# Linear attention beside weight products: a head's small TensorE work in seven groups instead of fifteen half steps

## The chip, the core and the metric

The kernel runs on one core of one Trainium2 chip. The metric is the device time of one execution in microseconds (us). Engines are named as in the profile: PE is TensorE's matmuls, PEld its weight loads, DVE VectorE, ACT ScalarE, POOL GpSimd, SP SyncE, whose queue issues most DMAs. A line such as L543 is line 543 of the kernel before; the change keeps the line numbers.

## The reference

One step of a hybrid decoder layer for 528 prompt tokens (512 and 16 learned meta tokens) and 32 sample tokens (8 sequences of 4), in float32, with a model width of 1024:

```
h = x + 0.5 * rms_norm(swiglu(rms_norm(x, ffn1_pre_g), ...), ffn1_post_g)
proj = rms_norm(h, mix_pre_g) @ w_in
q_a, k_a, v_a, gk_low, r_a, q_b, k_b, v_b, gate_a, gate_b = split(proj)
g = log_sigmoid(gk_low @ w_gk2 + b_gk) / 16
o_a, s_new = gla_branch(q_a, k_a, v_a, g, s0)       # linear attention, 4 heads
o_a = rms_norm(o_a, gla_norm_g) * silu(r_a)
o_b = sb_attend(q_b, keys, vals, sb_bias)           # stick-breaking attention, 16 heads
m = sigmoid(gate_a) * (o_a @ w_o_gla) + sigmoid(gate_b) * (o_b @ w_o_sb)
h = h + rms_norm(m @ w_out, mix_post_g)
y = h + 0.5 * rms_norm(swiglu(rms_norm(h, ffn2_pre_g), ...), ffn2_post_g)
```

The change touches only the linear attention (GLA). A head has 128 key and 256 value columns; tokens go in chunks of 64:

```
b = cumsum(g) in the chunk
q_in, k_in, k_end = q * exp(b), k * exp(-b), k * exp(b_last - b)
o = tril(q_in @ k_in.T) @ v + q_in @ S          # S: the state ahead of the chunk
S = exp(b_last) * S + k_end.T @ v
```

The 8 sample sequences do the same with their own states, which are inputs and outputs.

## The kernel before, in words

Activations lie turned (features on partitions, 560 token columns: 512 prompt, 32 sample, 16 meta). Every weight product is done as three matmuls: weights and activations are split in a high and a low part, and high x high, high x low and low x high are summed in PSUM (L728, L729, L731 in `tile_steps`). One **half step** is one of eight blocks of 128 input rows, over two halves of the tokens: six matmuls. After each half step `step()` runs what has come due in a list `todo`; `later(n, f)` puts `f` there for n half steps on. Everything small is put between the half steps in this way.

Over the four heads the kernel runs this loop: 16 half steps per head, eight for the head's queries and eight for its keys.

```
for hd, head in enumerate(HEADS):
    if hd:
        for n, f in HEADS[hd - 1].pieces():
            later(n + (hd == 1), f)
    ...
    if hd < 3:
        gla_gates(hd + 1, GATES, (0, 2, 3, 6))
    later(ROWS, head.rows)
    later(ROWS + 1, head.rows_out)
```

So in the loop of one head the **pieces** of the head ahead of it run, at the half steps of the table `OFF`. Head 0's pieces run one half step later than the table says. Head 3's pieces run in the first twenty half steps of the attention, whose Pair 0 makes its queries and keys there (eight half steps each).

The pieces that matter here, with the PE lines: scores of the prompt (L480, L483), `turned` (transposes of the keys, L437, L440), `sample_scores` (L511), `souts` (sample outputs from the old states, L531), `state0` to `state2` (L456, L459), `sums0` and `sums1` (L499, L502: a head's output), `sample_sum` (L560, L561), `sstate0` to `sstate3` (sample states, L543), and `turn0` to `turn2` (transposes of the normalised output, L592, L595). The names with `_out` read a product out of PSUM, on ACT (copies and scaled copies, L446, L465, L487, L513, L537, L601, L604) or DVE (the states, L175). `norm` squares and sums the outputs (ACT, L574, L577, L578), and `normed` scales them (ACT, L584).

Two more sets of small work stand in the loop. `head.rows` turns the head's values into rows (L377, L381, three PSUM tiles), and `rows_out` reads them out (ACT, L390, L393). `gla_gates` prepares the decay of the next head: `ranks` (two products, L312, read out on ACT, L313), `logs` (ACT, L317, L318), `sums` (DVE, a scan, L324), `exps` (ACT, L333 to L335). L706 and L1006 on ACT and the subtractions of `lo` on DVE split the coming weights. L2448 on ACT (`sums_hi`) casts sums of activations that are read back from DRAM.

**What sets the order.** PE, DVE, ACT and POOL run in the order in which the program's text emits instructions; SP's queue is ordered by a scheduler. PSUM has eight banks: four, by turns, for the weight products (`ps("acc")`), and a pool of **four buffers** for all small products (`ps()`). A new small tile takes the buffer of the fourth tile before it, and its first matmul waits until that has been read out. SBUF is one arena of 150 units; each `take` gets the next place from the byte table `PLACES`, so a changed order needs a new table.

Of the kernel before, what the change touches and what calls it, by code (L numbers as in the profile page):

```python
# [50 lines left out]


PLACES = bytes.fromhex("""
1e1218555a06420c505e52908e8070488a7a7e667668946a3264868c4c7c6038842a883462283c742672240a544e6e000292042c4a6c78823e2c
103c383a363047412d54565a0a5808443e424660067c8c0c34882c4c26247262842a742e1e0200146e824a786c123016921a36226a664890947a
32683c8e1e1880408a5a701003254e64277e86360e1a050428761b3e8a1f3a2318535c1c64360265700019260c0d4e1b017176283b5a64180038
3924231e0270190c1a36770d4e1876535b04013822715a5d641f1e0c1a707718100219384e712176645c1e0c5a702353100077183971763b6421
1e0c4e705323105a380c1a717776183a64651e23703818534e100e0c7684946c90788e6458468274167c7a4c500a88183c123008684a8c442c48
2e9270747a242a361e2c004c5a5d4823502e2036424b222a1e214b4d222a4c202d50511e4b5150224d1f201e212400301e50181c224b38373b36
393a19181b82667468603c5c14123e160690625a42501c442e4618887a84802d1b7e76947857153f6961673d928c0a72221e08200d4a13758317  # L60
49704c484b4d5d548e865c8a6e566a0e2d6c0c2c7c401910645570801a2a18847a54585c57562d888978795494725856768c0a2c187e9220221e
0428887824269046003234304e743a6862186053146612023b364a4c3f3e0848162c8209395c1e9238787e2a5a3626765618424c3c245d685428
4a60538c48666394881a14623f3e3a72501c22291e045d926078384a30342a2c7e58680a234e905c486654823a8c08282409636294885b551674
4604480032222047535a3e601e7802382e4a50665d429236194e3a5c764c9063088c82091c625e5672943c745b182e3846025406287e78926636
262458304c4a6888901676631214343a5b4e2b193802302a4e460a08573644555854423a3430061902265b2b425534522438503b262a060a5430
1b364e3a02192450570844425b2b19364e3402525618080a4630242e26292a2c4250380654025b1942242e34572938521a1c2c36024e30502a06
0a2d5b5d083418582c2a42245b072e38245256291c1806342a503a02542608240a4e3028504345341a3628065b2b4e420a303a0656072c2a3738
241c1934265402283a0845365c305e432e1a24454e37075b30585642062a2c1843191b4536383a5434025e5c1d4f565158282e0a0618424e5b08
0230024345560642262434580a36545c5e3a381c34360a1a58062e2c3a184f515e06323058011a54004a4c5c185e5a76622a28604a44423a3856
3e4e460234081c62560a60763663064a4c32625c525036185a5e320002463a441d08364a38421c4c345c0604621c080676604c56440a185c3a5a  # L70
1c0832065e424438585c08301a360a3a4c1c4656544b1a3208344a5d5c3022061e5848204a4442385c3a340b1a460a44080642304c1c32480a1e
203a54585632481a4a2c34634476602a246150280a26020462060801004460522200762e30634c1c02184e3e5a604246621a4a4c635e004d0405
18026260364b44764a4d395a18006e64108a1612687c787e6a740c7a408e8c88707284576726941e926d3406083266800a2c4a37829150140e4c
668648206c54828356242a28903a36573c8c60623e3d662d82804a37670822762c6e8e64661e339226670635949532080b8872706655847a0774
54610c0d41403f7e68426f0a778d658f46588a0706080b16124f747c3830548a104c3a780e423648866c267a142a9084822e5a1a24804a7e7288
683462662c2001187092527658604e5450563e466e0c7a5b8e1d65641a1e1c8c320822245a4243065f7a943d0402203c46181c26648f451e0008
225c1a03441f4006233c0a8f478e2028642400422202441c433c40235a03041a64245d0b5c0a461e5f42008f8e653e5a3d20040b64400226245c
4625416544428f3c0a8e40210222645c0425652400448f3c208e47400a0241465c5d5e24648e668874606c386834842e7e8a042c901800200e76
3c827c5430620a48725c0846108636784e5e06042818261e015c245a064600035c25282700245a05290403260424030025292826274206544e04
40033e241d28041a3c002c52137a8c18261c  # L80
""")


# [53 lines left out]
def hybrid_step(  # L137
# [15 lines left out]
    V, S, G, T = nc.vector, nc.scalar, nc.gpsimd, nc.tensor  # L153
# [20 lines left out]
    def stt(out, a, s, b, op0, op1):  # L174
        V.scalar_tensor_tensor(out=out, in0=a, scalar=s, in1=b, op0=op0, op1=op1)  # L175
# [125 lines left out]
    class Gates:  # L301


        def __init__(self, hd):
            self.hd = hd
# [39 lines left out]
    OFF = ((3, "scores spread"), (4, "scores_out turned"), (5, "turned_out souts sample_scores"), (6, "souts_out state0 skeys0"),  # L345
# [3 lines left out]

    class Head:  # L350


        def __init__(self, hd):
            self.hd, self.km, self.px = hd, {}, {}

        def load(self):

# [92 lines left out]
        def state(self, n):  # L450

            p = ps()
            if n == 0:
                self.owner = [take(512) for _ in range(3)]
                self.st = [self.owner[(j + 1) // 2][:, 256 * ((j + 1) % 2) : 256 * ((j + 1) % 2) + 256] for j in range(-1, 4)]
                T.matmul(p[:, :256], self.tl[NS:NTL, 256:384], self.tl[NS:NTL, :256], start=True, stop=True)  # L456
# [129 lines left out]

        def out_turned(self, e):

            p = self.po = ps()
            if e < 2:  # L590
                for j in range(4):
                    T.transpose(p[:, P * j : P * j + P], self.on[j // 2][:, 256 * (j % 2) + P * e : 256 * (j % 2) + P * e + P], ident)  # L592
            else:
                for e in range(2):
                    T.transpose(p[:, NS * e : NS * e + NS], self.on[2][:NS, P * e : P * e + P], ident[:NS, :NS])  # L595

        def out(self, e):
            hd, p = self.hd, self.po
            if e < 2:
                oa[hd, e] = take(NP + NS)  # L600
                S.activation(oa[hd, e][:, :NP], p, AF.Copy, scale=g_gla[:, e : e + 1])  # L601
            else:
                for e in range(2):
                    S.activation(oa[hd, e][:, NP:], p[:, NS * e : NS * e + NS], AF.Copy, scale=g_gla[:, e : e + 1])  # L604
                give(*self.on)
                for e in range(2):
                    later(1, lambda e=e: nc.sync.dma_start(oa_dram[2 * hd + e], oa[hd, e]))
                    later(6, lambda e=e: give(oa.pop((hd, e))))

        def pieces(self):  # L610
# [154 lines left out]
    def later(n, f):  # L765
        todo.append([n, f])
# [748 lines left out]
    with tc.manual_schedule(engines={E.PE, E.DVE, E.Activation, E.Pool}):  # L1515
# [277 lines left out]
        p = ps()  # L1793
        for j in range(5):
            n = P if j < 4 else NTL
# [702 lines left out]
    with tc.manual_schedule(engines={E.PE, E.DVE, E.Activation, E.Pool}):  # L2498
# [8 lines left out]
        starts, n = {}, -MIX0  # L2507
# [49 lines left out]
        for pr in range(8):  # L2557
            now, n, after = Pair(pr), BEGIN[pr + 1], BEGIN[pr + 2] if pr < 7 else BEGIN[8] + 18
# [25 lines left out]
        n, w0 = BEGIN[8], Weights(0)  # L2584
# [16 lines left out]
        n = 0  # L2601
# [29 lines left out]
        n = 8 * len(PAGES)  # L2631
# [43 lines left out]
        n = 0  # L2675
# [126 lines left out]
```

## Time and profile before

| | us |
|---|---|
| median of 3 runs | 1482.35 (1481.65 to 1482.51) |
| the profiled execution | 1483.2 |
| its span | 1481.5 |
| granted TensorE clock, mean | 0.999 |
| POOL busy in the span | 86.6 |
| mean DMA rate over the span | 127 GB/s |

The profile's page comes from one execution, 0.85 us above the median; its span is 1.7 us shorter than its time. The span is the frame of all instruction rows below, which give a start and a duration in us. PE's durations overlap, since matmuls are pipelined: the time from one start to the next is what a matmul takes. ACT and DVE instructions overlap by a little. The four heads' loops and the first half steps of the attention, which the change touches, lie from about 457 to 580 us.

### The profile page before, as it was taken

The numbers are of one execution on the slowest core, as the hardware profiler recorded it, in microseconds if no ns is written. First come the engines' busy times: TensorE is split into PE (matmuls) and PEld (weight loads), VectorE is DVE, ScalarE is ACT, GpSimd is POOL, SyncE is SP. The second block draws the span as 40 slices with busy tenths as digits, with TensorE's granted clock in tenths as the row PEclk, the third lists the DMA queues.
The fourth block names the chain that finished last, engine by engine and source line by source line (L and its number), as shares of the span: only waits on it lengthen the run. The fifth ranks groups of instructions, "written<-read, shape, count | busy, mean of one in ns | idle before, by whom it ended". The sixth has DMA issues, their size and how long they took to land.

```text
span 1481.5 us, 29805 instructions
## 1 busy us (share of the span) xinstructions
PE 1472.6 (99%) x11825; PEld 1426.8 (96%) x11825; DVE 1097.5 (74%) x1844; ACT 818.8 (55%) x1537; POOL 86.6 (6%) x175
## 2 busy tenths in 40 slices
PE   9999999999999999999999999999999999999998
PEld 8999999999999889999998999999999999999998
DVE  5888888855677866988887754776577888889544
ACT  7455545533565557777776544644564554545334
POOL 2000000000000111412211000000000000000000
PEclk9999999999999999999999999999999999999999
DMA  8133333324665787568687757335531333333243
GB/s 254 44 100 92 100 94 100 90 79 128 179 133 130 180 164 162 115 116 154 148 141 168 238 130 212 100 93 156 164 104 51 104 95 110 96 104 88 85 141 123
DMA packets 288541, 187.61 MB, mean 127 GB/s; under 512 B 10988, under 2 KB 266674, under 8 KB 288402
## 3 DMA queue, kind: packets, MB, share of 16 engines
q1 hardware_dynamic: 280706, 181.97, 46.5%
q0 software_dynamic: 7680, 3.74, 2.3%
q8 instruction: 93, 1.52, 0.4%
q14 instruction: 46, 0.38, 0.1%
q10 hardware_dynamic: 16, 0.00, 0.0%
HBM read 160.63 MB, written 25.03 MB: 125 GB/s over the span
## 4 chain that ended last, share of the span: by engine, by line
PE 95%; DVE 2%; ACT 1%; DMA 1%; issue 0%; DVEq 0%; SPq 0%; ACTq 0%
PE acc L1302 8%; PE acc L1301 8%; PE acc L1300 8%; PE acc L741 7%; PE acc L744 6%; PE acc L742 6%; PE acc L728 5%; PE acc L729 5%; PE acc L731 5%; PE acc L1079 4%; PE acc L1081 4%; PE acc L1080 4%; PE acc L1242 2%; PE acc L1239 2%; PE acc L1240 2%; PE ps L2105 1%
## 5 line engine op out<-in xcount | busy, mean ns | idle before, releaser
L172 DVE TENSOR_TENSOR room<-room,room 128x560 fp32r<-128x560 f32 (+14 forms) x464 | 300.9, 667 | 85.2 <-ACT room L1059 17.7
L172 DVE TENSOR_TENSOR lo<-raw,hi 128x1024 fp32r<-128x1024 f32 (+1 forms) x207 | 248.6, 1202 | 76.6 <-ACT hi L1006 39.3
L1302 PE MATMUL acc<-room,lo 128*128 128x280 f32 (+1 forms) x896 | 259.6, 290 | 0.0
L1300 PE MATMUL acc<-room,hi 128*128 128x280 f32 (+1 forms) x896 | 259.1, 289 | 0.0
L1301 PE MATMUL acc<-room,hi 128*128 128x280 f32 (+1 forms) x896 | 259.1, 289 | 0.0
L1006 ACT CAST hi<-raw 128x1024 fp32r<-128x1024 f32 x114 | 119.5, 1052 | 143.5 <-PE acc L1301 49.0
L728 PE MATMUL acc<-room,hi 128*128 128x280 f32 x608 | 173.1, 301 | 0.3 <-DVE room L175 0.3
L1300 PEld LDWEIGHTS acc<-room,hi 128*128 128x128 f32 x896 | 168.8, 188 | 0.0
L1302 PEld LDWEIGHTS acc<-room,lo 128*128 128x128 f32 x896 | 168.7, 188 | 0.0
L1301 PEld LDWEIGHTS acc<-room,hi 128*128 128x128 f32 x896 | 168.5, 188 | 0.0
L729 PE MATMUL acc<-room,hi 128*128 128x280 f32 x608 | 163.5, 288 | 0.0
L1079 PE MATMUL acc<-room,hi 128*128 128x280 f32 x476 | 141.7, 298 | 1.1 <-ACT acc L1069 1.0
L172 DVE TENSOR_TENSOR lo<-room,hi 128x1024 fp32r<-128x1024 f32 x106 | 101.2, 955 | 53.0 <-ACT hi L1006 52.8
L1081 PE MATMUL acc<-room,lo 128*128 128x280 f32 (+1 forms) x476 | 138.5, 291 | 0.0
L1080 PE MATMUL acc<-room,hi 128*128 128x280 f32 (+1 forms) x476 | 138.2, 290 | 0.0
L706 ACT CAST hi<-raw 128x1024 fp32r<-128x1024 f32 (+1 forms) x93 | 93.6, 1007 | 77.6 <-issue 20.4
L1006 ACT CAST hi<-room 128x1024 fp32r<-128x1024 f32 x106 | 89.1, 840 | 81.7 <-PE acc L1301 60.6
L731 PE MATMUL acc<-room,lo 128*128 128x280 f32 x608 | 125.7, 288 | 0.0
L728 PEld LDWEIGHTS acc<-room,hi 128*128 128x128 f32 x608 | 114.4, 188 | 5.3 <-issue 3.9
L729 PEld LDWEIGHTS acc<-room,hi 128*128 128x128 f32 x608 | 114.6, 188 | 0.3
L741 PE MATMUL acc<-room,hi 128*128 128x280 f32 (+2 forms) x388 | 110.7, 295 | 0.0
L742 PE MATMUL acc<-room,hi 128*128 128x280 f32 (+2 forms) x388 | 108.8, 290 | 0.0
(412 smaller groups left out, 3588.2 us busy)
## 6 DMA issues: line engine op xcount, KB each, us to landing
raw<-in_w_in_dram SPq DMA_DIRECT2D x68, 256.0 KB, 5.2
raw<-in_ffn_w_gate_dram SPq DMA_DIRECT2D x64, 256.0 KB, 3.1
raw<-in_ffn_w_up_dram SPq DMA_DIRECT2D x64, 256.0 KB, 3.3
raw<-in_ffn_w_down_dram SPq DMA_DIRECT2D x36, 448.0 KB, 3.8
raw<-in_w_in_dram SPq DMA_DIRECT2D x29, 512.0 KB, 6.9
out_dram<-room SPq DMA_DIRECT2D x36, 256.0 KB, 4.0
room<-in_cache_k_dram SPq DMA_DIRECT2D x32, 256.0 KB, 5.1
room<-in_cache_v_dram SPq DMA_DIRECT2D x32, 256.0 KB, 5.9
```

Of the source, the lines that this page charges most:

```text
L172: (eng or V).tensor_tensor(out=out, in0=a, in1=b, op=op)
L728: T.matmul(acc[h][:, :w], hi[k], act.get(k, h, w)[0], start=(k == order[0]), stop=False, skip_group_check=True)
L729: T.matmul(acc[h][:, : wid[h]], hi[k], a[h][1], start=False, stop=False, skip_group_check=True)
L731: T.matmul(acc[h][:, : wid[h]], lo[k], a[h][0], start=False, stop=(k == order[-1]), skip_group_check=True)
L741: T.matmul(acc[h][:nw, : wid[h]], wh, a[h][0], start=(k == 0), stop=False)
L742: T.matmul(acc[h][:nw, : wid[h]], wh, a[h][1], start=False, stop=False)
L1006: S.copy(hi[:, :kt], src)
L1079: T.matmul(x[:, :n], hi, act_[k][0][:, :n], start=(first and k == 0), stop=False, skip_group_check=True)
L1081: T.matmul(x[:, :w], lo, act_[k][0][:, :w], start=False, stop=(k == 3), skip_group_check=True)
L1300: T.matmul(x[:, :QW], hi, act[k][0], start=(first and k == 0), stop=False, skip_group_check=True)
L1301: T.matmul(x[:, :QW], hi, act[k][1], start=False, stop=False, skip_group_check=True)
L1302: T.matmul(x[:, :QW], lo, act[k][0], start=False, stop=(k == 3), skip_group_check=True)
```

## The change

The table `OFF` is written anew: PE work of the pieces stands at half steps 5, 8, 11, 13, 16 and 19 (with the rows and the gates' products, seven groups a head, where there were fifteen half steps with such work). `GATES` moves the next head's gates from half step 6 to 16, so that their products fall at the end of the loop and the rest of the gates in the next one. Since several state tiles and several turned tiles are now open at once, `ps_` and `po` become dictionaries. `PLACES` is a new table of SBUF places (its lines are left out).

```diff
-    OFF = ((3, "scores spread"), (4, "scores_out turned"), (5, "turned_out souts sample_scores"), (6, "souts_out state0 skeys0"),
-           (7, "state_out0 state1 skeys1"), (8, "state_out1 state2 sums0 skeys2"), (9, "state_out2 skeys3 sstate0"),
-           (10, "sums1 sstate_out0 sample_sum"), (11, "sstate1"), (12, "norm0 sstate_out1"), (13, "norm1 normed0 sstate2"),
-           (14, "normed1 sstate_out2"), (15, "sstate3"), (16, "sstate_out3 turn0"), (17, "out0 turn1"), (18, "out1 turn2"), (19, "out2"))
+    OFF = ((4, "spread"), (5, "scores turned"), (6, "scores_out turned_out"), (8, "sample_scores souts state0 state1 skeys0"),
+           (9, "state_out0 state_out1 souts_out skeys1"), (11, "state2 sums0 sstate0"), (12, "state_out2 sstate_out0 skeys2"),
+           (13, "sums1 sample_sum sstate1 skeys3"), (14, "norm0 sstate_out1"), (15, "norm1 normed0"), (16, "normed1 sstate2 sstate3"),
+           (17, "sstate_out2 sstate_out3"), (19, "turn0 turn1 turn2"), (20, "out0 out1 out2"))
...
-            self.hd, self.km, self.px = hd, {}, {}
+            self.hd, self.km, self.px, self.ps_, self.po = hd, {}, {}, {}, {}
...
-            self.ps_ = p
+            self.ps_[n] = p
...
-                S.copy(self.st[0], self.ps_[:, :256])
+                S.copy(self.st[0], self.ps_[0][:, :256])
...
-                stt(self.st[j + 1], self.st[j], self.dec[:, 16 + j : 17 + j], self.ps_[:, 256 * (j % 2) : 256 * (j % 2) + 256],
+                stt(self.st[j + 1], self.st[j], self.dec[:, 16 + j : 17 + j], self.ps_[n][:, 256 * (j % 2) : 256 * (j % 2) + 256],
...
-            p = self.po = ps()
+            p = self.po[e] = ps()
...
-            hd, p = self.hd, self.po
+            hd, p = self.hd, self.po[e]
...
-    GATES, ROWS, EARLY = 6, 1, {7: 2}
+    GATES, ROWS, EARLY = 16, 1, {7: 2}
```

Three places show how the order moves. In the rows stand the line, the operation, what is written, what is read and the shape; `ps_` with a number is one PSUM tile of the four buffers, `room` a place of the arena, `x2` the same twice.

PE at the end of the loop in which head 0's pieces run (from the last sample state to the rows of the next head), before:

```order
L543 MATMUL ps_5696<-room_46_611 128x256 x2
...
L592 MATMUL ps_5715<-ident,room_97_5315 128x128 x2
...
L377 MATMUL ps_5725<-ident,room_9_92 128x128
...
L377 MATMUL ps_5730<-ident,room_9_92 128x128
...
L381 MATMUL ps_5735<-ident,room_9_92 48x128
...
L592 MATMUL ps_5745<-ident,room_97_5315 128x128 x2
```

The same place of the change; between the second L312 and the first L543 stand six main matmuls, and none behind them up to L381:

```order
L312 MATMUL ps_5669<-room_33_296,wgk_106 128x280
L312 MATMUL ps_5672<-room_33_296,wgk_106 128x280
...
L543 MATMUL ps_5690<-room_38_338,room_101_5622 128x256 x2
L543 MATMUL ps_5693<-room_38_338,room_101_5622 128x256 x2
L377 MATMUL ps_5701<-ident,room_78_4589 128x128
...
L377 MATMUL ps_5706<-ident,room_78_4589 128x128
...
L381 MATMUL ps_5711<-ident,room_78_4589 48x128
```

The last two sample states and the gates' products of the next head have moved to the three rows tiles: seven PSUM tiles with one half step of main matmuls among them, where four stood together, and `turn0` and `turn1` (L592) have moved behind them.

ACT at the same place, from the scaling of head 0's outputs (L584) to the reading of the values' rows (L390), before:

```order
L584 ACTIVATE room_97_5315<-ps_5586,st_0_5263 128x256 x2
L584 ACTIVATE room_96_5310<-ps_5587,st_0_5263 128x256 x2
L584 ACTIVATE room_98_5485<-ps_5633,st_0_5263 32x256
L706 CAST hi_5699<-raw_5340 128x1024
L601 ACTIVATE room_5_73<-ps_5715,gains 128x512
L390 ACTIVATE room_78_4316<-ps_5725,rcol 128x256 x2
```

And in the change:

```order
L584 ACTIVATE room_88_5294<-ps_5601,st_0_5259 128x256 x2
L584 ACTIVATE room_91_5454<-ps_5602,st_0_5259 128x256 x2
L313 ACTIVATE room_72_4301<-ps_5669,gains 128x280
L313 ACTIVATE room_72_4301<-ps_5672,gains 128x280
L706 CAST hi_5676<-raw_5323 128x1024
L584 ACTIVATE room_97_5544<-ps_5634,st_0_5259 32x256
L317 ACTIVATE room_95_5514<-room_95_5514 128x560
L318 ACTIVATE room_95_5514<-room_95_5514 128x560
L390 ACTIVATE room_95_5514<-ps_5701,rcol 128x256 x2
```

The gates' read-outs and logarithms (L313, L317, L318) have come in ahead of the rows' read-out (L390), and the cast of the next weights (L706) stands ahead of the sample rows' L584.

DVE at Pair 0's keys in the attention, where head 3's pieces end (L175 reads out the sample states, L1960 and the L172 behind it make the key parts, L1965 copies the sample keys), before:

```order
L175 SCALAR_TENSOR_TENSOR room_68_3355<-room_68_3355,room_78_4316,ps_6553 128x256 x2
L175 SCALAR_TENSOR_TENSOR room_68_3355<-room_68_3355,room_78_4316,ps_6579 128x256 x2
L172 TENSOR_TENSOR room_46_611<-room_78_4316,room_46_611 64x512
L1960 CAST room_113_6570<-room_98_5485 64x528
L172 TENSOR_TENSOR room_55_1071<-room_98_5485,room_113_6570 64x528
...
L172 TENSOR_TENSOR room_107_6312<-room_98_5485,room_113_6570 64x528
L1965 COPY room_81_4592<-room_98_5485 128x32
```

And in the change:

```order
L175 SCALAR_TENSOR_TENSOR room_91_5454<-room_91_5454,room_72_4301,ps_6531 128x256 x2
L172 TENSOR_TENSOR room_111_6554<-room_74_4441,room_111_6554 64x512
L1960 CAST room_111_6554<-room_7_75 64x528
L172 TENSOR_TENSOR room_106_6300<-room_7_75,room_111_6554 64x528
...
L172 TENSOR_TENSOR room_103_5877<-room_7_75,room_111_6554 64x528
L1965 COPY room_8_76<-room_7_75 128x32
L175 SCALAR_TENSOR_TENSOR room_88_5294<-room_88_5294,room_72_4301,ps_6582 128x256 x2
L175 SCALAR_TENSOR_TENSOR room_71_4267<-room_71_4267,room_72_4301,ps_6585 128x256 x2
```

The read-outs of the last two sample states have moved from ahead of the key parts to behind them.

More of the change, by code (lines that the diff above doesn't have):

```diff
@@ L53 @@
 PLACES = bytes.fromhex("""
[L54 to L77, printed above, removed]
@@ L78 @@
-4625416544428f3c0a8e40210222645c0425652400448f3c208e47400a0241465c5d5e24648e668874606c386834842e7e8a042c901800200e76
-3c827c5430620a48725c0846108636784e5e06042818261e015c245a064600035c25282700245a05290403260424030025292826274206544e04
-40033e241d28041a3c002c52137a8c18261c
+48005a262c1f3012163447923c720e0c5054568010528462948e6a7a7c6e8c0682364e648a58387e863e1c2b2a746c8860187042081a90783842
+66247668060a2b393a224026201e2c2a127c2e7a6e8a8c3058647e4e3836863e821c88704a43481a6c7460907800021804075a5e687650665456
@@ new lines @@
+526280940c723c8e4a426a93124d284b13060a375a84250e0c312472085c1430334692426b4a44116a3b3948845a273726360e246b30925e385f
+104c3b12840d395d4a446a265a6b465c5e36920e323a3b930c123126144a30856a384b5a5e92930f103a84260c460e8532304a5a6a0f4b921014
+93265e8446850c324a5a0e924b936a108485284a260c2946045c925a5e826a947c88628c8460700e905664164a788a4e80542a667402207e0048
+421c1e5818244c644412361601000d3014103248640c31421610111213311415420c4514101213450c161517143612484e522f100c241a1c2a82
+602d644527747e5a5c621e105e7c8a90186c024452084200062827922b2e720c8f7658407a4f5b83611d5f6356543c701f883e22241b758b7d7f
@@ new lines @@
+5d6a91111021314e0c9427846e2678860a8c680b0e80336a64328e6630244e72924f26500a0b3377767b7a54264e5658320a703c883e40764c48
+28367a384a16132a043a6c1c1e02157c2c62745c90837e5a8a1b602e221a898846123c2082525e1e403e385044245c2c36107c76237458624c90
+8a3254157e5a701b127b260a7a1a46024208034e281e307c40203e4c62563c1c82588874220490323a4a8a23705a7e605561066c1b1a46480842
+775c2e131e2a2c125417827a5e90267c3015327488768a4a5a707e18495852500328480408246090107c020506220a38005556260b88741a6230
+363a155a4270448a403c6c1d76462058484f0624563e400b005552504d22323c34304920400424263e58370631485636203c004d503028265522
@@ new lines @@
+040258410a0806203624004e483c55310a080230384d3c26040650524e05203222363e40083455004e480a323a4d2031403c3000022628344804
+06534a5856243e3732304e0648550422205308303e3c4d24363834062028002655023a31363858244c402204314e553602080a3048533e3c504e
+5126044c202824380036223b0434322606403a224f55003136484a4e30080a555826562228203e243432383a05524f22264a4c304000554f3732
+3c2240563c580855484a2634060a243a30203e362808020400384c522634061e3220133a000b30380a7a5a241654046c82504e3432407a263c56
+201c15065c02823e6c582834363f5a32130a56161e2236243e5404820a153c7a14403226365c130256165a06084013587a6c285a0234243c5440
@@ new lines @@
+1404563e162636280034323a0214305a5c381354043d023258563c34122a3a3e2c36345e00262e3c5a1256023028033258263e5d3a345e54382a
+2e362c0204005e5c30520a12542813504c7b4e081e206c328348567a822638581c7a3a2206128313326c4a28305c2426123e82391332347a387b
+3e3a14165c3882127a6d7b423c308c0d1a6c7084641888746678607a685510727c906e5187806a76928e2a040200635e2c5c2e39868a1e208e4c
+5048627e0a368694388a0f57084e50510d280c128c22952e54862c5a945d064a2614821695016a802a943a240300045d396e92907695367c7372
+38787960056869889419296113178d15701c6c4b8325077264187a506c4e5a84744c8e1e52387e627c0a445e102056580e8a2a3e366a08544886
@@ new lines @@
+809088946e322b3c927612262270821428160130064a005c1c422a5b8c781a6824381847342f363245600c022c46002e3c40785c1a1c5a318c3e
+4237433579334618455c04362c782a023b1a8c30353133002f432d3237795c5e36382b4742783c308c431a358d2a1c322d3704795c473c5a3b42
+2e367846342a8c1a2c798d37395c3642463b3c3d04348c1a3778798d392e363b3d3c042c4642448c887822281e480e82747c807a869013700a6e
+3662843c947e50268a5654526c1a181c00584e5e803090125a505c542a7057564e525e81805f54905c915d504e5c805e815f5d90914e2a303880
+010580407036903c03005c3e0e6474706086
```

## The prediction

> **What bounds the kernel now.** I read the page's first and fourth part, then the idle time of PE by releaser, then the busy time by stretches over the four heads, and last the single instructions of those stretches.
>
> ```profile
> PE 1472.6 (99%) x11825; PEld 1426.8 (96%) x11825; DVE 1097.5 (74%) x1844; ACT 818.8 (55%) x1537; POOL 86.6 (6%) x175
> ...
> PE 95%; DVE 2%; ACT 1%; DMA 1%; issue 0%; DVEq 0%; SPq 0%; ACTq 0%
> ```
>
> TensorE is busy 99% of the span and carries 95% of the chain that ended last. It works in program order, so whatever time it gains or loses anywhere is the program's. The other engines matter only where PE waits for them. Here is all of that waiting that the view of waits lists near or over 0.3 us:
>
> ```profile
> PE acc L1533 <- DVE own L276: 1.1, 1, 1.1
> PE acc L1079 <- ACT acc L1069: 1.0, 1, 1.0
> PE acc L744 <- DVE lo L172: 0.5, 1, 0.5
> ...
> PE acc L728 <- DVE room L175: 0.3, 1, 0.3
> ```
>
> Only the last lies in the heads' stage. The change can therefore win back almost no waiting, and it can add some. The stretches of the heads (engine busy times, then the granted clock) say the same:
>
> ```profile
> 476.50:500.00 23.50, 23.50 (x170) 20.20 (x170) 20.11 (x45) 14.13 (x37) 2.55 (x6) 1.00 0.62 154
> 500.00:525.00 25.00, 25.00 (x185) 21.83 (x183) 19.73 (x45) 15.76 (x44) 2.61 (x8) 1.00 0.70 178
> 552.00:580.00 28.00, 28.00 (x208) 24.66 (x206) 17.28 (x38) 17.78 (x46) 4.78 (x8) 1.00 0.86 163
> ```
>
> PE has no gap in them. DVE (third time, 20.11 of 23.50) and ACT (fourth, 14.13) have little or moderate slack and must now do their evacuations in bursts.
>
> **What grouping saves on PE.** The same matmuls run, so only the borders of a group can become cheaper. These rows (start, duration) are around two groups at the end of head 0's pieces:
>
> ```profile
> 498.48 0.42 PE L731 MATMUL acc<-room,lo 128*128 128x280 f32 x2
> 498.74 0.40 PE L543 MATMUL ps<-room 128*128 128x256 f32 x2
> 498.98 0.29 PE L728 MATMUL acc<-room,hi 128*128 128x280 f32 x1
> ...
> 499.49 0.42 PE L731 MATMUL acc<-room,lo 128*128 128x280 f32 x2
> 499.75 0.60 PE L592 MATMUL ps<-ident,room 128*128 128x128 f32 x4
> 500.19 1.04 PE L377 MATMUL ps<-ident,room 128*128 128x128 f32 x8
> 501.06 0.38 PE L381 MATMUL ps<-ident,room 128*48 128x128 f32 x2
> ```
>
> Durations overlap, so I count from start to start. Two L731 take 0.26 before the L543 and 0.26 before the transposes, which is two of the usual 0.13. Two L543 take 0.24 before the main matmuls go on. Four transposes take 0.44 beside a main product and eight take 0.87 behind other transposes, so 0.11 each either way. A border between full-size tiles is free to 0.01 us, and putting two groups together saves nothing. One half step of six main matmuls takes 0.77 (498.74 to 499.75, less 0.24). It is different where the tile's size changes:
>
> ```profile
> 507.18 0.41 PE L731 MATMUL acc<-room,lo 128*128 128x280 f32 x2
> 507.52 1.07 PE L531 MATMUL ps<-room,room 128*32 128x256 f32 x16
> 508.41 0.22 PE L511 MATMUL ps<-room,room 128*32 128x32 f32 x2
> 508.57 0.40 PE L728 MATMUL acc<-room,hi 128*128 128x280 f32 x1
> ...
> 509.16 0.41 PE L731 MATMUL acc<-room,lo 128*128 128x280 f32 x2
> 509.51 0.69 PE L456 MATMUL ps<-room 16*128 16x256 f32 x2
> ```
>
> The two L731 take 0.34 and 0.35 here, 0.08 to 0.09 more. In the change L511 and L531 (32 columns) stand straight ahead of L456 (16 rows), so one way out to the full size and one way back in disappear per head: 2 x 0.09 to 0.10 x 4 heads = **0.8 us saved**, between 0 and 0.8, since the change from the one odd size to the other may cost as much as one of the two. [...]
>
> Two small waits go as well. The L728 wait quoted above goes because head 0's queries come nine DVE instructions earlier when the gates of the next head have left the middle of the loop: 0.3 us by its row (the start of that matmul is 0.45 late, which I take). The other is within the group of sums below, a quarter of a microsecond, because its state is a step older: 0.25. Saved in all 0.8 + 0.45 + 0.25 = **1.5 us**.
>
> **What the bunching adds.** There are four PSUM buffers for all small products. A new tile waits until the fourth tile back has been read out, and PE stands still behind it with all main matmuls. Before, a half step opened one to four tiles. Now the gates' two (L312), the last two sample states (L543 twice) and the next head's three tiles of rows (L377 twice, L381) open with one half step of main matmuls among them: seven tiles for four buffers. Which read-out each waits for follows from the order; the times come from these rows of ACT and PE, at the sums and norm of head 0:
>
> ```profile
> 491.14 2.13 PE L502 MATMUL ps<-room,room 128*128 128x256 f32 x8
> ...
> 494.30 0.40 PE L728 MATMUL acc<-room,hi 128*128 128x280 f32 x1
> ```
> ```profile
> 492.26 0.38 ACT L574 ACTIVATE room<-ps 128x256 f32<-128x256 f32 x1 [0.79 <-PE ps L502]
> ...
> 495.75 1.88 ACT L584 ACTIVATE room<-ps,st 128x256 f32<-128x256 f32 x5
> ```
> ```profile
> L706 ACT CAST hi<-raw 128x1024 fp32r<-128x1024 f32 x10 | 10.4, 1043 | 3.3 <-PE acc L729 3.3
> L390 ACT ACTIVATE room<-ps,rcol 128x256 f32<-128x256 f32 x16 | 6.3, 478 | 1.2 <-PE ps L377 1.2
> L584 ACT ACTIVATE room<-ps,st 128x256 f32<-128x256 f32 x16 | 6.2, 471 | 0.0
> ...
> L313 ACT ACTIVATE room<-ps,gains 128x280 f32<-128x280 f32 x6 | 2.6, 492 | 3.7 <-PE ps L312 3.6
> ...
> L317 ACT ACTIVATE room<-room 128x560 f32<-128x560 f32 x3 | 2.0, 673 | 2.9 <-DVE room L175 2.9
> L318 ACT ACTIVATE room<-room 128x560 f32<-128x560 f32 x3 | 2.0, 671 | 0.1
> ```
>
> *End of head 0's pieces.* Zero is the start of L502. The group ends at 3.16. With sstate1 (0.24) and two half steps (1.54) the gates' L312 starts at 4.94. ACT begins its five L584 at 4.61 and, at 1.88 for five, starts one each 0.36; the second ends at 5.44 and the fourth at 6.16. Consecutive ACT instructions overlap by 0.1, so each adds its mean less 0.1. The second L312 wants its buffer at 5.06 and gets it at 5.44 (wait 0.4). One half step later sstate2 and sstate3 go without a wait (6.33 to 6.81). The first L377 waits for the second L313, done at 6.16 + 2 x 0.4 = 6.96 (0.15). The second L377 wants a buffer at 7.40, but that one is read by the sample rows' L584, which stands behind the cast L706: 6.96 + 0.94 + 0.36 = 8.26 (0.86). L381 wants one at 8.70, which the two L390 of the first rows tile free; they stand behind L317 and L318: 8.26 + 2 x 0.57 + 2 x 0.4 = 10.2 (1.5). Together **2.9 us**. At least 1.0, if L706 and the gates' logs should find their place earlier, and 3.5 without the overlaps.
>
> *At souts of head 0*, in the middle of the loop, L531 waits for ACT's L487, which stands behind the gate's three exponentials now that these fall early in the next loop: I take **0.5**, a quarter of the way from 0 to 2.0, which is all three at L317's 0.67, since two half steps lie between.
>
> *End of head 1.* The same crowd, but without the shift by a step that only head 0 has: the first waits (0.3) and L381, now on DVE's sstate_out2, which stands behind the gate's combining instruction that needs L313 (0.9): **1.2**, from 0 to 2.9. Head 2 has no gates behind it: 0.
>
> *Head 3, beside Pair 0 of the attention.* The read-out of sstate2 (sstate_out2, on DVE) was ahead of Pair 0's key parts and is now behind them, and turn2 (L595) reuses its buffer. The rows:
>
> ```profile
> 577.31 0.39 ACT L1947 COPY room<-acc 128x280 f32<-128x280 f32 x1 [0.49 <-PE acc L731]
> ```
> ```profile
> 580.74 0.18 DVE L1965 COPY room<-room 128x32 f32<-128x32 f32 x1
> ```
> ```profile
> L2448 ACT CAST room<-room 128x560 fp32r<-128x560 f32 x5 | 3.1, 662 | 0.0
> ```
> ```profile
> L175 DVE SCALAR_TENSOR_TENSOR room<-room,room,ps 128x256 f32<-128x256 f32 x32 | 13.9, 476 | 11.8 <-PE ps L543 11.8
> ```
>
> From L502's start again: ACT's fourth L584 ends at 6.16, two L2448 (1.2) and the sample L584 (0.4) follow, and L1947 starts at 7.7. From L1947 to the end of L1965 it takes 3.6 (577.31 to 580.92), and two L175 take 0.9: the buffer is free at 12.2. PE is there at 3.40 + 3 x 0.77 + 0.48 (two sample states) + 3 x 0.77 + 0.88 (turn0, turn1) = 9.4. Wait 2.8; 3.4 if a cast L1932, moved ahead of the sample norm, takes its 0.6 there too. I take **3.1**, from 1.0 (if ACT were as early as before) to 3.4.
>
> **Sum.** 2.9 + 0.5 + 1.2 + 3.1 = 7.7 added, 1.5 saved: +6.2. The profiled execution took 1483.2 us, 0.85 above the median of 1482.35; 1483.2 + 6.2 = 1489.4 there, so **1488.5 us** as a median. Everything else (no more PE instructions, other addresses in SBUF, the same DMAs) I cost at nothing, covered by a PE that is never idle in these stretches; where a weight came late, the row of L744 above prices it at 0.5 a time.
>
> **Rivals.**
>
> *No measurable change.* About 0.2%, 3 us, is what a measurement here can tell from no change. The waits are chained: one that PE pays early gives ACT and DVE time, and the next one shrinks. With the lower ends (1.0 + 0 + 0 + 1.0, less 1.5) the time is 1482.9; with half of my sum of waits, 1484.7. ACT's 14.13 of 23.50 speaks for it, ACT's strict order against. **1484**, chance 0.25.
>
> *Faster.* The mechanism would be a cost at each border of a group. Fifteen groups become seven, so eight per head, 32, and 64 borders go. With b a border, the time is 1482.35 - 1.5 - 64 b plus the waits. It decides for faster if b exceeds 0.025 and the waits are none, or 0.15 and they are as I say. The rows give 0.01 at most at full size. With 0.03 and no waits it is **1479**; chance 0.08.
>
> *Slower still.* The waits let the clock fall. No row here shows a clock below 1.00, and none a wait of this length between matmuls. If one head's 25.00 us of PE work ran at 0.9, that would cost 2.8 us, 5.6 for two: **1494**; chance 0.05. [...]
>
> **How the numbers follow.** My forecast has 0.62, the rivals 0.25, 0.08 and 0.05. The range goes from no wait with all that is saved (1482.35 - 1.5 = 1480.9, a little under it 1480.5) to the upper ends of the waits, 3.5 + 2.0 + 2.9 + 3.4 = 11.8, less 0.7 where the tile changes save nothing: 1493.5. Slower by over 0.2% (above 1485.3) has the forecast and the last rival, 0.67; within, 0.25; faster, 0.08.
>
> **What would show it.** In the profile after, PE's waits should list L381 and L377 on ACT's L390 and L584, L312 on L584, and L595 on DVE's L175, each in tenths up to 3 us, at the loop ends and at Pair 0's keys; the granted clock should stay 1.00; L531 to L456 should have no full-size matmul between. I am wrong if these waits are missing, or if PE's own busy time falls by more than 1 us without them.

## The result and the profile after

| | before | after |
|---|---|---|
| median, us | 1482.42 (1481.65 to 1482.70, 6 runs) | 1491.27 (1489.78 to 1491.99, 6 runs) |
| the profiled execution, us | 1483.2 | 1491.25 |
| its span, us | 1481.5 | 1489.6 |
| granted TensorE clock, mean | 0.999 | 0.998 |

The changed kernel is slower by 8.85 us. The ratio is 1.0058, with a 95% interval of 1.0045 to 1.0071. The direction and the range of the prediction held; the size was 8.85 where 6.15 was forecast.

These are the first and the fourth part of the page of after (busy time by engine; shares of the chain that ended last):

```profile
PE 1473.9 (99%) x11825; PEld 1426.9 (96%) x11825; DVE 1097.4 (74%) x1844; ACT 816.7 (55%) x1537; POOL 89.5 (6%) x175
...
PE 94%; ACT 3%; DVE 2%; DMA 1%; issue 1%; DVEq 0%; ACTq 0%; SPq 0%
```

PE's share of the chain has gone from 95% to 94%, and ACT's from 1% to 3%. PE now waits for ACT's read-outs. The idle time of PE by releaser, after (us in total, times, longest):

```profile
PE ps L595 <- DVE room L175: 2.5, 1, 2.5
PE ps L1614 <- DVE room L1613: 2.1, 2, 1.8
PE ps L381 <- ACT room L390: 1.3, 1, 1.3
...
PE ps L377 <- ACT room L584: 0.6, 1, 0.6
PE ps L381 <- DVE room L175: 0.6, 1, 0.6
...
PE ps L312 <- ACT room L584: 0.3, 1, 0.3
```

L1614 lies at the program's start and not in the changed code; in before it is listed with 0.4, a row outside the heads that the prediction's list leaves out (as it does L872's 0.4). It comes back below. The other five are the waits for PSUM buffers that were forecast, each behind the engine and line named. The wait of L728 behind DVE's L175, 0.3 before, is no longer listed. The stretches of before, and two more at Pair 0's keys (PE, PEld, DVE, ACT, POOL busy, granted clock, DMA share, GB/s):

```profile
476.50:500.00 23.50, 23.13 (x167) 19.89 (x167) 18.23 (x40) 12.52 (x37) 2.48 (x6) 1.00 0.59 139
500.00:525.00 25.00, 23.07 (x171) 19.78 (x171) 20.07 (x44) 13.25 (x34) 2.72 (x7) 1.00 0.63 160
552.00:580.00 28.00, 28.00 (x204) 24.15 (x203) 15.92 (x36) 15.91 (x50) 4.72 (x8) 1.00 0.89 182
584.00:588.00 4.00, 1.48 (x12) 1.20 (x11) 3.83 (x9) 3.95 (x9) 0.00 (x0) 1.00 0.66 156
588.00:592.00 4.00, 4.00 (x22) 4.00 (x21) 3.94 (x7) 0.78 (x3) 0.00 (x0) 0.57 0.75 265
```

PE has gaps in the first two stretches and in the fourth. In the fifth it has none, but its clock is granted at 0.57. That is the part no term of the sum held; I call it the slow stretch. PE's rows there, from the end of L595's wait:

```profile
587.02 0.30 PE L595 MATMUL ps<-ident,room 32*128 32x32 f32 x2 [2.52 <-DVE room L175]
587.25 0.39 PE L728 MATMUL acc<-room,hi 128*128 128x280 f32 x1
...
589.14 0.43 PE L728 MATMUL acc<-room,hi 128*128 128x280 f32 x1
589.37 0.43 PE L729 MATMUL acc<-room,hi 128*128 128x280 f32 x1
...
591.94 0.33 PE L728 MATMUL acc<-room,hi 128*128 128x280 f32 x1
```

A main matmul takes 0.23 from start to start (589.14 to 589.37) where it takes 0.13 elsewhere, for 14 matmuls, and then the usual pace is back.

**Where the 8.05 us between the two profiled executions went.** The main matmuls are the same in both kernels and come in the same order, so the start of the same one can be compared. Of before, three of them: one ahead of the heads, the one that follows L595 in after, and the one 24 main matmuls further on:

```profile
455.82 0.29 PE L741 MATMUL acc<-room,hi 128*128 128x280 f32 x1
...
580.86 0.29 PE L728 MATMUL acc<-room,hi 128*128 128x280 f32 x1
...
583.95 0.29 PE L728 MATMUL acc<-room,hi 128*128 128x280 f32 x1
```

In after they start at 457.41, 587.25 and 591.94; the last main matmul of all starts at 1478.37 instead of 1470.33. So after is late by 1.59 ahead of the heads, 6.39 behind them, 7.99 behind the slow stretch and 8.04 at the end. The heads cost **4.80**, the stretch at half clock **1.60**, and 1.59 lay there before the changed code ran at all.

### The profile page after: what moved, and what is told of

It is laid out like the page before. It is cut to its first block, busy times and chain, and to the rows that moved or that the text cites. A ratio compares the mean times of both kernels' runs of the same rounds, so it can differ in the third digit from the quotient of the medians.

```text
span 1489.6 us, 29774 instructions
## 1 busy us (share of the span) xinstructions
PE 1473.9 (99%) x11825; PEld 1426.9 (96%) x11825; DVE 1097.4 (74%) x1844; ACT 816.7 (55%) x1537; POOL 89.5 (6%) x175
## 4 chain that ended last, share of the span: by engine, by line
PE 94%; ACT 3%; DVE 2%; DMA 1%; issue 1%; DVEq 0%; ACTq 0%; SPq 0%
PE acc L1300 8%; PE acc L1302 8%; PE acc L1301 8%; PE acc L741 6%; PE acc L744 6%; PE acc L742 6%; PE acc L728 5%; PE acc L731 5%; PE acc L729 5%; PE acc L1079 4%; PE acc L1081 4%; PE acc L1080 4%; PE acc L1242 2%; PE acc L1239 2%; PE acc L1240 2%; PE ps L2105 1%
## 5 line engine op out<-in xcount | busy, mean ns | idle before, releaser
L172 DVE TENSOR_TENSOR room<-room,room 128x544 fp32r<-128x544 f32 (+14 forms) x465 | 301.0, 667 | 75.7 <-ACT room L808 16.9
L172 DVE TENSOR_TENSOR lo<-raw,hi 128x1024 fp32r<-128x1024 f32 (+1 forms) x207 | 248.3, 1200 | 77.7 <-ACT hi L1006 40.2
L728 PE MATMUL acc<-room,hi 128*128 128x280 f32 x608 | 170.9, 298 | 0.0
L172 DVE TENSOR_TENSOR lo<-room,hi 128x1024 fp32r<-128x1024 f32 x106 | 101.2, 955 | 52.3 <-ACT hi L1006 52.1
L706 ACT CAST hi<-raw 128x1024 fp32r<-128x1024 f32 (+1 forms) x93 | 93.7, 1007 | 79.1 <-issue 21.6
L728 PEld LDWEIGHTS acc<-room,hi 128*128 128x128 f32 x608 | 115.2, 189 | 1.6 <-issue 1.2
```

The costliest lines, as they stand in the source:

```text
L172: (eng or V).tensor_tensor(out=out, in0=a, in1=b, op=op)
L728: T.matmul(acc[h][:, :w], hi[k], act.get(k, h, w)[0], start=(k == order[0]), stop=False, skip_group_check=True)
```

## The experiments

Two questions stood. Are the waits caused as forecast, by what stands ahead of a read-out in ACT's and DVE's order, and not by the grouping as such? And where do the other 4 us come from? The runs e1 to e4 were made on one chip, with a median of before of 1482.48 (22 runs), and e5 to e8 on another, with 1482.33 (15 runs). Where an order changes, the table of places is solved again if it must be (at most 95 of 1526 bytes); e1, e2 and e5 have the change's own. "Heads" below is the lateness gained between the two matmuls of before at 455.82 and 580.86, as above.

### e1: the last turn two half steps later

```diff
-        for n, f in HEADS[3].pieces():
+        for n, f in HEADS[3].pieces(OFF[:-2] + ((19, "turn0 turn1"), (20, "out0 out1"), (21, "turn2"), (22, "out2"))):
```

> The change, with head 3's turn2 two half steps later (at 21, out2 at 22). The wait of L595 for DVE's L175 was 2.5 us; two half steps of main matmuls (0.77 each) now pass before it, so about 1.0 us should be left. Theory: that one long wait also caused the stretch at half clock behind it (588.6 to 592 us, 14 matmuls and more at 0.233 instead of 0.129), which should then be gone: 1491.3 - 1.5 - 1.6 = 1488.2. Rival: the half clock comes from Pair 0's work or from all idle time together: it stays, and the time is 1489.8.

Measured: 1486.95 (1486.59 to 1488.67), ratio 1.0031 (1.0019 to 1.0042). L595's wait fell from 2.5 to 1.0:

```profile
PE ps L595 <- DVE room L175: 1.0, 1, 1.0
```

That is less waiting by 1.5, but 4.3 us less time than after. Part of the rest is the clock: in the six executions that were only timed it was 1.000 in the mean, and one slow stretch costs 1.6. For the other 1.2 us no trace shows a cause. The profiled one, the slowest, has a slow stretch at another place, behind the waits of L377 and L381 at the end of head 0:

```profile
500.00:503.50 3.50, 1.56 (x13) 1.02 (x11) 3.23 (x8) 3.47 (x8) 0.00 (x0) 1.00 0.11 40
503.50:507.00 3.50, 3.50 (x17) 3.49 (x18) 3.41 (x8) 1.43 (x4) 0.00 (x0) 0.53 0.44 150
```

So the stretch does not belong to L595. It can follow several shorter waits too (here PE is busy 1.56 of 3.50 us). It need not: after has the same waits at the same place, at a clock of 1.00 from 500 to 508 us, and e2 has them too, but its heads cost 2.23 in all: the waits that were left (6.3 less 2.6, measured below) less the net saving of 1.5 make 2.2, which leaves no room for a stretch's 1.6.

### e2: the sample states read out ahead of Pair 0's key parts

```diff
-        for n, f in HEADS[3].pieces():
+        for n, f in HEADS[3].pieces(OFF[:-4] + ((16, "normed1 sstate2 sstate3 sstate_out2 sstate_out3"),) + OFF[-2:]):
```

> The change, with head 3's sstate_out2 and sstate_out3 emitted at half step 16, ahead of Pair 0's key parts. Theory: the order on DVE is the whole cause of the L595 wait, so it vanishes with the half clock behind it: 1491.3 - 2.5 - 1.6 = 1487.2. Rival: ACT's late norm holds turn2 as well (its input is the sample rows' L584), and most of the wait stays: 1490 or more.

Measured: 1485.99 (1485.46 to 1487.48), ratio 1.0025 (1.0015 to 1.0035). L595 is gone from the list of waits, and at Pair 0's keys PE is full at full clock:

```profile
584.00:588.00 4.00, 4.00 (x33) 4.00 (x32) 3.89 (x8) 3.97 (x10) 0.00 (x0) 1.00 0.69 226
```

Only DVE's order differs: head 3's `turn` pieces still stand in one group of three. Its heads cost 2.23 instead of 4.80. This shows the cause of the largest wait, DVE's read-out behind the key parts. Between the two profiled executions lie 5.45 us: 2.57 from the heads, 1.5 from the slow stretch and 1.3 from the start, which was late in after's profiled execution and not in e5's.

### e3: the gates back at half step 6

```diff
-    GATES, ROWS, EARLY = 16, 1, {7: 2}
+    GATES, ROWS, EARLY = 6, 1, {7: 2}
```

> The change, with the next head's gates back at half step 6 (GATES = 6; 18 places of the table differ). Theory: at the end of head 0's pieces the L312 wait (0.47 late) goes, the second L377 waits some 0.4 and L381 some 0.4 instead of 0.76 and 1.5, and the L381 wait of head 1 (0.74) goes: about 2.5 us less, less the 0.45 that moving the gates had saved ahead of head 0's queries: 1489.3. The L595 wait and the half clock stay. Rival: the sample states moved together are the cause, not the gates: 1491.

Measured: 1488.69 (1488.14 to 1489.27), ratio 1.0044 (1.0028 to 1.0061); heads 4.43. The end of the loop is relieved in part, for L381 no longer waits but L377 still does, and two waits have come elsewhere: L312 in the middle of the loop of head 0's pieces (at 482.30) and L502 at head 1's sums (at 523.37):

```profile
PE ps L595 <- DVE room L175: 2.4, 1, 2.4
...
PE ps L502 <- DVE room L175: 0.9, 1, 0.9
...
PE ps L377 <- ACT room L584: 0.6, 1, 0.6
PE ps L312 <- ACT room L313: 0.6, 1, 0.6
```

Moving the gates changes where PE waits and hardly how much (4.43 against 4.80). The heads were expected to cost 2 us less, and that failed. The time came near what was expected for other reasons: in this execution L595 waited 2.4 us and no slow stretch followed (the clock stayed 1.00 from 580 to 592 us), and the start was level with before (0.21 late).

### e4: only the pieces of one tile size put side by side

The kernel before, with `souts` and `sample_scores` moved to `state0`'s half step and the scores to `turned`'s; the gates one half step later, so that four buffers do.

```diff
-    OFF = ((3, "scores spread"), (4, "scores_out turned"), (5, "turned_out souts sample_scores"), (6, "souts_out state0 skeys0"),
-           (7, "state_out0 state1 skeys1"),
+    OFF = ((3, "spread"), (4, "scores turned"), (5, "scores_out turned_out"), (6, "sample_scores souts state0 skeys0"),
+           (7, "souts_out state_out0 state1 skeys1"),
...
-    GATES, ROWS, EARLY = 6, 1, {7: 2}
+    GATES, ROWS, EARLY = 7, 1, {7: 2}
```

> The kernel before, with only those groups put together that share an odd tile size or border on one: scores with the transposes (L480, L483, L437) at half step 4, sample_scores and souts with state0 (L511, L531, L456) at 6, and the gates at 7; all else as before. By the rows of before and after, a head saves 0.20 and 0.09 us of tile changes and no wait is added: 4 x 0.29 = 1.2 us, 1481.2. Rival: borders between full tiles cost too, or the later scores add waits: 1482.4 or more.

Measured: **1480.27** (1479.68 to 1481.07), ratio 0.9986 (0.9977 to 0.9996), faster than before by less than 0.2%, and so faster than after too. No wait for a small tile was added; the heads gain 2.05. The tiles of odd size now touch:

```profile
506.42 0.20 PE L511 MATMUL ps<-room,room 128*32 128x32 f32 x1
506.45 1.03 PE L531 MATMUL ps<-room,room 128*32 128x256 f32 x13
507.42 0.69 PE L456 MATMUL ps<-room 16*128 16x256 f32 x2
```

By the trace this is about all that grouping has to give: 2.05 less the two small waits that went (0.45 and 0.25) is 1.35, or 0.34 a head, of which 0.29 stand at these tiles start to start. It needs none of the bunching.

### e5: the change once more, unaltered

> The change once more, unaltered. In the first profile of the change the start (up to 35 us) took 1.4 us longer than in the kernel before, and a stretch at half clock stood behind the L595 wait; in two kernels with the same start and the same table the start took as long as before. Theory: both come and go by execution: the median stays within 1489.5 and 1491.5, executions lie in two groups 1 to 1.6 apart, and the start of this profile differs from the first. Rival: they belong to the change: start +1.4 and half clock again, all executions near 1491.

Measured: 1490.85 (1488.97 to 1491.33), ratio 1.0055 (1.0041 to 1.0069). Its profiled execution (1489.76) has the same waits but starts level with before: the matmul at 455.82 comes at 456.05, the one behind L595 at 585.88, the one 24 further on at 590.60 and the last at 1476.83. That is 0.23, then 4.79 in the heads, 1.63 at half clock, and −0.15 to the end. So heads and slow stretch repeat to 0.03 us, and the 1.59 ahead of the heads belongs to the execution (e1's profiled one has 0.87 there). Its row is L1614's 1.8, near the start.

Over the eleven executions of after and e5, the time goes with the mean clock: 1488.97 at 1.000, 1490.05 at 0.999, 1489.76 to 1491.46 (five) at 0.998, 1490.85 to 1491.99 (four) at 0.997. That suggests executions without a slow stretch, with one and with more than one. Both traces have one; no trace shows two. A mean of 0.999 alone settles nothing: e1's profiled execution has it with a stretch and before's without, since the clock also fell where the work ran out at the end (0.78 from 1475 to 1481 us in before, with PE busy 1.26 of 6.00).

### e6: e2, and the gates' logarithms behind the rows' read-out

```diff
-                gla_gates(hd + 1, GATES, (0, 2, 3, 6))
+                gla_gates(hd + 1, GATES, (0, 3, 4, 6))
```

> The change with the read-outs ahead of Pair 0's keys (as e2_readout_ahead, 1486.0), and with the gates' logarithms (L317, L318) a half step later, so that on ACT they stand behind the rows' read-out (L390, L393). Theory: ACT's order makes the L381 wait of 1.34 us; L390 now runs 1.15 us sooner and about 0.3 is left: 1486.0 - 1.1 = 1484.9. Rival: the wait is made by what is further ahead (L313, L706, the sample rows' L584), and L381 stays at 1.0 or more: 1486.

Measured: 1484.44 (1483.77 to 1484.99), ratio 1.0014 (1.0005 to 1.0024). ACT at the end of head 0, after:

```profile
500.76 1.07 ACT L706 CAST hi<-raw 128x1024 fp32r<-128x1024 f32 x1
501.69 0.46 ACT L584 ACTIVATE room<-ps,st 32x256 f32<-32x256 f32 x1
502.06 0.66 ACT L317 ACTIVATE room<-room 128x560 f32<-128x560 f32 x1
502.75 0.67 ACT L318 ACTIVATE room<-room 128x560 f32<-128x560 f32 x1
503.32 1.55 ACT L390 ACTIVATE room<-ps,rcol 128x256 f32<-128x256 f32 x4
```

And PE beside it, after:

```profile
502.21 0.66 PE L377 MATMUL ps<-ident,room 128*128 128x128 f32 x4 [0.60 <-ACT room L584]
...
504.20 0.40 PE L381 MATMUL ps<-ident,room 128*48 128x128 f32 x2 [1.34 <-ACT room L390]
```

PE in e6:

```profile
500.70 0.66 PE L377 MATMUL ps<-ident,room 128*128 128x128 f32 x4 [0.60 <-ACT room L584]
501.41 0.40 PE L381 MATMUL ps<-ident,room 128*48 128x128 f32 x2
```

From the second L377 to L381 it was 1.99, and is now 0.71: 1.28 less. The edit moves DVE's scan (L324) half a step later as well, but L381's buffer is freed by L390 on ACT, and L390 stood behind two logarithms of another tile, which nobody was waiting for yet. The heads cost 0.91, against e2's 2.23. With two read-outs ahead in their engines' order, four fifths of the heads' cost are gone, though the groups are the same.

### e7: head 3's turns one half step sooner

Meant to lengthen the wait of L595, to see whether the slow stretch grows with it.

```diff
-        for n, f in HEADS[3].pieces():
+        for n, f in HEADS[3].pieces(OFF[:-2] + ((18, "turn0 turn1 turn2"), (19, "out0 out1 out2"))):
```

> The change, with head 3's three turns a half step sooner (18, read-outs at 19). The buffer for turn2 comes free at the same time, so PE reaches L595 0.77 us sooner and waits 3.3 instead of 2.5 us; the end of the stage does not move. Theory: a longer wait brings the half clock behind it in every execution: 1491, in one group. Rival: the length of the wait does not matter to the clock: two groups as for the change, median as there or 1489.7.

Measured: 1491.63 (1488.88 to 1492.67), ratio 1.0059 (1.0044 to 1.0074). The wait grew, and its releaser is now ACT:

```profile
PE ps L595 <- ACT room L601: 3.9, 1, 3.9
```

A wait of 3.3 was expected. The slow stretch stayed what it was: 13 slow matmuls. One execution of the four took 1488.88 at a mean clock of 0.999, against 1491.33 to 1492.67 at 0.997 and 0.998. That suggests that even this wait, the longest here, does not always bring the stretch on, though that execution has no trace; that every execution would have it was expected, and is not borne out. The longer wait (3.9 us, against 2.5 in after, which has 14 such matmuls) made the stretch no longer.

### e8: the gates alone, in the kernel before

```diff
-    GATES, ROWS, EARLY = 6, 1, {7: 2}
+    GATES, ROWS, EARLY = 16, 1, {7: 2}
```

> The kernel before, with only the gates moved (GATES = 16). The two L312 then come a half step ahead of one turn and the rows, with the sample states already out. Theory: without the sample states and turns bunched there, the move costs about nothing: 0.45 saved ahead of head 0's queries, 0 to 1 us of waits at L381 for L601 behind L317 and L318: 1482.0 to 1483.0. Rival: the gates' place is itself the cause of the waits at the end of the loops: 1484.5 or more.

Measured: 1490.30 (1489.10 to 1491.68), ratio 1.0056 (1.0041 to 1.0072). The expected time failed by over 7 us. The heads cost 6.18, 5.4 of it at one place in each of three loops that the expectation took to be covered, the sample outputs at half step 5:

```profile
PE ps L531 <- ACT room L446: 2.8, 1, 2.8
PE ps L531 <- issue: 1.7, 1, 1.7
...
PE ps L531 <- ACT room L238: 0.9, 1, 0.9
```

ACT there (e8) shows why:

```profile
480.94 0.67 ACT L333 ACTIVATE room<-room 128x560 f32<-128x560 f32 x1 [1.98 <-DVE room L324]
...
482.78 0.58 ACT L446 COPY room<-ps 128x512 f32<-128x512 f32 x1
483.26 0.29 ACT L238 CAST room<-room 32x128 fp32r<-32x128 f32 x1
```

ACT waits 1.98 for DVE's scan, runs three exponentials, and only then reads out the turned keys (L446), whose buffer PE needs. With the gates at 16 that work falls into the early half steps of the next loop. The change has moved `souts` from step 5 to 8, and there the same exponentials cost PE 0.27. So it is the later first groups that make the late gates bearable. Alone, the late gates cost about as much as the whole change.

## Why the prediction was right, and where its size was off

**PE in program order, and waits for the four buffers: right.** Each wait that the forecast said the profile would list was found behind the engine and line named. Two were taken away by a change of order alone, of a read-out (e2) or of what stood ahead of one (e6), with PE's groups as they were, by about the wait's own size: 2.57 and 1.32 in the heads, for listed waits of 2.5 and 1.3. That shows the cause of these two. For L312 and L377 of head 0 and L381 of head 1 (0.47, 0.76, 0.74) it is read from the order and the trace, and no run took them away by themselves. Two small terms of the forecast did not come (0.15 at the first L377, 0.3 at the start of head 1's end), and the 0.27 of L531 shows start to start only: the view of waits has no row for it.

**What grouping saves: right.** Start to start, with the main matmuls taken off, the sample products and first states take 0.20 less per head in after, and the scores and turned keys 0.09: 1.16 for four heads. The two small waits are gone too, 0.70 together. That is 1.86, where 1.5 was forecast; the heads' net, 6.3 us of waits (below) less 4.80 of cost, is 1.5, so some 0.35 was lost again in places too small to name. That a change of tile size costs is borne out by e4, which changes only such neighbours, and gains 2.05 in the heads. That a border between full-size tiles costs nothing rests on the rows of before (0.01 us at most) and on this sum, which leaves no gain over for it.

**The waits, 7.7 forecast, measured 6.3**, start to start as in the forecast:

| place | forecast | measured |
|---|---|---|
| end of head 0's pieces | 2.9 | 2.7 (L312 0.47, L377 0.76, L381 1.50) |
| `souts` of head 0 | 0.5 | 0.27 |
| end of head 1 | 1.2 | 0.74 |
| head 2 | 0 | 0 |
| `turn2` at Pair 0's keys | 3.1 | 2.6 |

All four are a little under the forecast and within its bounds. How dear the `souts` term can be, e8 shows: 2.8 at that line for one wait.

**The clock: wrong.** The forecast said that the granted clock would stay 1.00, and gave the rival in which the waits let it fall a chance of 0.05. It fell to 0.5 (the rival's 0.9 no run shows), but for 3.4 us and not for a whole head, so it cost 1.6 a time and not 2.8 or 5.6: the rival had the mechanism, and not its size. It is the only mechanism of the change that I found missing from the sum. Before's own trace had the sign: its rows in the heads' stage show 1.00, but where PE runs out of work at the end (busy 1.26 of 6.00 us from 1475 to 1481) the clock is granted at 0.78.

**From the profiled execution to the median: wrong by 0.85.** The forecast took 0.85 off, because before's profiled execution lay that far above its median. That of after lies at its median (1491.25 and 1491.27). In e5 it lies 1.1 below (1489.76 and 1490.85). Such an offset belongs to an execution and doesn't carry over.

The direction owes nothing to luck, since the heads alone cost 4.8. The size came as near as it did partly by errors of opposite sign: the heads were cheaper than forecast, and terms that the sum lacked made up for more than that. The miss of 2.77 us (1491.27 less 1488.5) is, by the profiled executions: 0.87 for this offset, −1.4 for the heads (4.8, not 6.2), +1.60 for the slow stretch, +1.59 for the lateness ahead of the heads, together 2.66. The fourth term differs by execution (e5 has 0.23, e1 0.87). In the median, further slow stretches in some executions may stand in its place: the clocks of 0.997 in four of eleven executions speak for that, but no trace shows it, and it stays open.

**Also open:** e2's median is 3.5 us above before's, while its heads cost 2.23 and the places' new table 0.3 by the matmul ahead of them. The 0.85 by which before's profiled execution lies above its median fits the gap, but what it consists of I could not find in the traces.

The faster rival fell: a border at full size costs nothing that the rows show, and no gain from the 64 removed borders is left in the sum. The rival of no measurable change was right about the chain of waits shrinking (6.3 of 7.7), but not down to half.

## What to carry to other kernels

Putting small matmuls together paid here only where neighbours then share an odd tile size; for full-size tiles the border was free to 0.01 us by the rows of before, and the bunch was paid for in PSUM buffers. Before bunching, count the tiles it opens against the pool, and for each tile beyond it look at what stands ahead of the freeing read-out in ACT's or DVE's order; moving that read-out ahead of work that nobody waits for yet removed most of the cost here. Where the sum holds waits like those that had a slow stretch behind them here (2.5 us at once in after, 0.6 and 1.3 close together in e1), add a possible slow stretch to it (1.6 us here); whether one came differed between the executions.

## What the runs showed of the hardware

- **The clock was granted at half behind some of the waits.** It stood at 0.50 for 3.41 us (after), with 14 matmuls at 0.23 us each instead of 0.13, and 1.60 us lost; e5 lost 1.63, and e7 has 13 such matmuls. It came behind single waits of 2.5 (after, e5) and 3.9 us (e7), and behind waits of 0.6 and 1.3 close together (e1). In after it began 1.3 us behind the main matmuls' return (587.25 to 588.60), in e1 within 0.3 us of it (503.66, with 0.23 from start to start from 503.96 on).
- **Where its steps lay in two traces.** In the clock's record of before the fall at the end lies 431 times 3.413 us behind the first entry. In that of after the stretch begins 171 times and ends 172 times 3.413 us behind the first entry, and the fall at the end lies 434 times behind it. The 3.41 us ahead of the stretch in after, and the stretch itself:

```profile
585.18:588.59 3.41, 1.57 (x12) 1.53 (x13) 3.36 (x9) 3.39 (x8) 0.00 (x0) 1.00 0.53 154
588.60:592.00 3.40, 3.40 (x17) 3.40 (x16) 3.34 (x6) 0.18 (x1) 0.00 (x0) 0.50 0.71 253
```

Ahead of two other stretches PE was busy 1.56 of 3.50 us (e1, 500.00 to 503.50) and 1.35 of 3.00 (e5, 584 to 587 us). The length of a wait alone does not tell whether a stretch comes: behind L595's 2.5 us one came in after and in e5, and behind its 2.4 us in e3 none, with PE busy 2.83 of the 4.00 us from 580 and 2.72 of the 4.00 from 584. Why is not shown. Nor does PE's busy time alone: e8 has 3.41 us with PE busy 1.49, less than the 1.57 of after, and the clock stayed 1.00 behind them:

```profile
479.11:482.52 3.41, 1.49 (x13) 1.25 (x11) 3.34 (x6) 1.58 (x3) 0.62 (x1) 1.00 0.25 77
482.52:485.94 3.42, 2.55 (x26) 1.80 (x26) 3.34 (x9) 1.47 (x6) 0.98 (x5) 1.00 0.39 78
```

- **How idle PE has to be is open.** It was not idle throughout ahead of the stretch in after (busy 1.57 of 3.41 us), and with a little less work in e8 (1.49 of 3.41) none came.
